# The order of the head work beside a hybrid encoder layer's dense matmuls, and where its short convolution is computed

## The chip, the cores and the metric

The kernel runs on one core of one Trainium2 chip. The metric is the device time of one launch in microseconds; below it, a profile of one execution tells where the time goes. TensorE (PE) does matmuls and transposes, VectorE (DVE) and GpSimd (POOL) elementwise work, ScalarE (ACT) activations and copies, and SyncE (SP) issues the transfers between the chip's memory and the core's. Each engine takes its own instructions in order and waits at one whose inputs are not there.

## The reference

One layer over a prompt of 2048 tokens and a sample group of 32 tokens with carried-in states; the model width is 1024, all values are float32.

```python
hn = rmsnorm(h, norm_mix)
qkv_pre, z, ba, u5, cc = split(hn @ w_in)
ya = gdn_mixer(...)        # delta rule: 4 heads x 128
yb = s5_mixer(...)         # diagonal state space, scan
yc = conformer_conv(...)   # gate, 31-tap causal conv, layernorm, silu
h = h + concat(ya, yb, yc) @ w_out
hf = rmsnorm(h, norm_ffn)
h = h + (silu(hf @ w1) * (hf @ w3)) @ w2
h = h + (p @ pe_w) * sigmoid(h @ pe_gate)
y = rmsnorm(h, norm_final)
```

`gdn_mixer` first passes q, k and v (1536 channels) through a causal convolution of width 4 and a silu, normalises q and k, and then runs a gated delta rule over chunks: within a chunk a triangular system is solved, from chunk to chunk a 128 x 128 state per head is carried. The kernel uses chunks (windows) of 128 tokens. All states are outputs too.

## The kernel before, in words

Tokens are taken in four blocks of 512; the last block also has the 32 sample tokens (544). All dense products are done as three passes of rounded parts: each operand is split into a high and a low part, and high x high, low x high and high x low are added up (`_dense`, line 122 of the profile: 24 matmuls of 512 columns for one 128-column tile of a weight with eight row tiles). `load_weight` loads a weight tile, ScalarE makes the high part (L94), GpSimd (for w3 VectorE) the low one (L98); the low parts are kept in device memory (L102), and later blocks load them (L93) instead of computing them.

**Phase A** (`PhaseA.block`, four blocks) computes the input projection, 22 weight tiles a block: first the two u5 tiles, then the conformer's gate and value (ccg, cca, two tiles each), twelve qkv tiles (`PhaseA.conv`), and four z tiles. The norm's factor comes late: its sums run beside the first tiles, and a broadcast of it over the partitions, `bc`, is made on TensorE after the first u5 tile (L134). Every result but u5's is multiplied by it when it leaves PSUM. `conv` writes a tile's product into `raw` (L615). For blocks 0 and 1 it then does the width-4 convolution at once (one ScalarE copy, L623, and three VectorE steps, L625) and the silu (L627, L628) and stores the result in `sild`; for blocks 2 and 3, which are in `G.raw`, it stores the raw rows.

**Phase F** (`PhaseF.block`, four blocks) does the output projection (8 tiles), the feed-forward part (22 hidden tiles of w1 and w3, L1194 to L1202; w2 in groups of four hidden tiles, L1216), the gated embedding (L1239 to L1241) and the final norm.

**The heads** are the work between the phases, one generator for each kind. `s5_init` prepares the constants of the state space. `gdn_of(b)` runs two delta-rule groups of two windows each for block b, and in block 3 a small third group for the sample. A group (`gdn_group`) loads its rows; for blocks in `G.raw` it does the convolution and silu itself (L887 to L892); then come the norms of q and k (L905), the products of keys (L933), the transposes of v (L957), a trip through device memory (`ud`, `cu`), 31 elimination steps of two small VectorE operations each (L980, L981), a trip back (`xd`, `X`), a VectorE transpose into `XT` (L990), two doublings on TensorE (L1011 q, L1024 z, L1042), and for each window the products with the state (L1054, L1067, L1074, L1081, L1082), and last the normalised output (L1107, L1108), stored to `mixT`. `conf_of(b)` is the conformer: 31 taps over two channel tiles, all on VectorE in one accumulator per tile (L822, L824), transposes (L835), layer norm, transposes back (L854). `s5_of(u)` does two blocks of the state space.

**What sets the order.** A generator yields between its parts. `dense` calls `step` with its columns, and each time STAGE columns of dense work have been issued, every chain in `G.chains` is advanced by one part; a `yield n` holds its chain for n parts. Chains share the right side of the memory: the pools of one kind reuse the space of another, so a kind starts when the one whose space it takes is finished. Phase A's block 0 is issued first; then a first chain is started: `s5_init`, `gdn_of(0)`, `conf_of(0)`. A second chain, `s5_of(0)`, starts before block 2. After phase A, `G.flush()` issues all that is left of the chains. In phase F one chain runs `conf_of(b)`, `s5_of` (at b = 2) and `gdn_of(b)` for b = 1, 2, 3, and before each F block a flush finishes what that block reads.

The program issued in this way is not yet the order on the engines. A planner with its own timing model orders each engine's instructions by priority and by when its model finds them ready: loads, evictions and splits go first ("first"), the dense matmuls and the heads share one lower priority ("later"), in which the place in the program counts.

```python
G.acc += cols
while G.acc >= STAGE:
    G.acc -= STAGE
    G.chains = [c for c in G.chains if advance(c)]
```

Of the kernel before, what the change touches and what calls it, by code (L numbers as in the profile page):

```python
# [8 lines left out]
F32 = mybir.dt.float32  # L9
F32R = mybir.dt.float32r  # L10
AF = mybir.ActivationFunctionType
# [5 lines left out]
P = 128  # L17
# [12 lines left out]
STAGE = 9216  # L30
# [541 lines left out]
class PhaseA:  # L572
# [60 lines left out]
    def block(self, b):  # L633
# [38 lines left out]

        for j in range(2):
# [3 lines left out]
            u = wp.tile([P, L5, n // L5], F32, tag="gacc", name="u5")  # L677
# [3 lines left out]
            if j == 0:  # L681

                with G.later():
                    bcast_cols(G, G.psN, "pn", rc, n, bc)
                    pb = G.psN.tile([P, 512], F32, tag="pn", name="ps_ba")
                    for w in range(4):
                        nc.tensor.transpose(pb[:, w * 16:(w + 1) * 16], fb[:, w * P:(w + 1) * P], G.ident[:16, :16])
                    if last:
                        nc.tensor.transpose(pb[:TS, 64:80], fb[:, BLK:n], G.ident[:16, :16])
                    pb3 = pb[:, :80].rearrange("p (w c) -> p w c", c=16)  # L690
                    ba = wp.tile([P, 4, 8], F32, tag="ba", name="ba")
                    bl = wp.tile([P, 5, 8], F32, tag="bl", name="bl")
                    nc.scalar.activation(bl[:, :4], pb3[:, :4, 8:], AF.Copy)
                    V.tensor_tensor(ba, pb3[:, :4, :8], bl[:, :4], op=ALU.add)
                    V.tensor_tensor(ba, ba, rc[:, :4, None].to_broadcast([P, 4, 8]), op=ALU.mult)
                    if last:
                        bad = wp.tile([TS, 1, 8], F32, tag="bad", name="bad", bufs=1)
                        nc.scalar.activation(bl[:TS, 4], pb3[:TS, 4, 8:], AF.Copy)
                        V.tensor_tensor(bad[:, 0], pb3[:TS, 4, :8], bl[:TS, 4], op=ALU.add)
                        V.tensor_scalar(bad, bad, rt, None, op0=ALU.mult)  # L700
                    gs = [gates(G, A, wp, G.psN, ba, b * 4, [P, 4, 8], "gp", G.tp_)]
                    if last:
                        gs.append(gates(G, A, wp, G.psN, bad, 0, [TS, 1, 8], "gd", G.td_))
                    for g in gs:
                        next(g)
# [96 lines left out]
def conformer_block(G, A, b, wp, pspool):  # L802
# [18 lines left out]
    for j in range(2):  # L821
        V.tensor_scalar(acc[:, j], xc[:, j, 0:W], cn_.w[:, j, 0:1], cn_.b[:, j:j + 1], op0=ALU.mult, op1=ALU.add)  # L822
        for t in range(1, TAPS):
            V.scalar_tensor_tensor(acc[:, j], xc[:, j, t:t + W], cn_.w[:, j, t:t + 1], acc[:, j], op0=ALU.mult, op1=ALU.add)  # L824
            if t % 6 == 0:
                yield 1
# [737 lines left out]
```

## Time and profile before

| what | us |
|---|---|
| median of three runs | 2949.75 (2946.05 to 2954.26) |
| the profiled execution | 2947.25 |
| its span, first to last instruction | 2945.4 |
| PE busy | 2769.4 |
| DVE busy | 1764.2 |
| ACT busy | 938.9 |
| POOL busy | 534.5 |
| mean granted TensorE clock | 0.969 |

The profile's times are microseconds from the first instruction; "mean" durations are nanoseconds. A row of a group reads: line, engine, operation, tile written <- tiles read, shape, xcount | busy, mean of one | idle time of the engine just before them and what ended it. A row of the timeline reads: start, duration, engine, line, operation, count, and in brackets how long the engine stood idle before it and for what. The table of busy times by stage gives the busy time of each engine in a stretch with the count of its instructions, then the granted clock and the share of the transfer engines. Matmuls overlap in the profile, so their mean duration is longer than the distance between two of them.

### The profile page before, as it was taken

The numbers are of one execution on the slowest core, as the hardware profiler recorded it, in microseconds if no ns is written. First come the engines' busy times: TensorE is split into PE (matmuls) and PEld (weight loads), VectorE is DVE, ScalarE is ACT, GpSimd is POOL, SyncE is SP. The second block draws the span as 40 slices with busy tenths as digits, with TensorE's granted clock in tenths as the row PEclk, the third lists the DMA queues.
The fourth block names the chain that finished last, engine by engine and source line by source line (L and its number), as shares of the span: only waits on it lengthen the run. The fifth ranks groups of instructions, "written<-read, shape, count | busy, mean of one in ns | idle before, by whom it ended". The sixth has DMA issues, their size and how long they took to land.

```text
span 2945.4 us, 40970 instructions
## 1 busy us (share of the span) xinstructions
PE 2769.4 (94%) x15300; PEld 2364.0 (80%) x15300; DVE 1764.2 (60%) x3933; ACT 938.9 (32%) x1409; POOL 534.5 (18%) x460
## 2 busy tenths in 40 slices
PE   7799999992999999799999999999999979999997
PEld 5678787992878878588788887778888869999997
DVE  8966737478675766966474664956374643333343
ACT  4243422221422222243332333342242423222232
POOL 5731213022332422441010010101010110000000
PEclk9899999995999999999999999999999979999998
DMA  6587767662654646487665565666555554555553
GB/s 221 168 291 263 237 213 222 196 197 80 228 173 167 205 157 212 136 282 212 205 199 177 191 193 175 233 203 181 177 187 176 186 192 155 179 175 172 172 183 106
DMA packets 278919, 565.32 MB, mean 192 GB/s; under 512 B 67344, under 2 KB 126880, under 8 KB 278576
## 3 DMA queue, kind: packets, MB, share of 16 engines
q1 hardware_dynamic: 278720, 562.70, 59.3%
q8 instruction: 121, 1.98, 0.3%
q14 instruction: 78, 0.64, 0.1%
HBM read 457.76 MB, written 104.25 MB: 191 GB/s over the span
## 4 chain that ended last, share of the span: by engine, by line
PE 69%; DVE 14%; DMA 8%; issue 5%; ACT 1%; SPq 1%; POOL 1%; DVEq 0%; ACTq 0%; POOLq 0%
PE ps_d L122 60%; DVE cacc L824 4%; DMA xk<-in_xT 1%; DVE cx L981 1%; DMA mixT<-zy 1%; DVE gacc L625 1%; PE ps_kk L933 1%; DVE ct L980 1%; PE ps_q L1011 1%; PE ps_z L1024 1%; DMA cu<-ud 1%; PE ps_o L1081 1%; PE ps_o L1082 1%; PE ps_vn L1067 1%; DVE hb L1216 1%
## 5 line engine op out<-in xcount | busy, mean ns | idle before, releaser
L94 ACT ACTIVATE wh_w<-wr_w 128x1024 fp32r<-128x1024 f32 (+1 forms) x272 | 281.2, 1034 | 766.2 <-PE ps_d L122 528.7
L122 PE MATMUL ps_d<-fah,wh_w 128*128 128x512 f32 (+1 forms) x1760 | 378.1, 354 | 6.7 <-DVE fa L1194 3.0
L122 PE MATMUL ps_d<-fal,wh_w 128*128 128x512 f32 (+1 forms) x1760 | 379.3, 354 | 0.0
L122 PE MATMUL ps_d<-fah,wl_w 128*128 128x512 f32 (+1 forms) x1760 | 377.8, 353 | 0.0
L122 PEld LDWEIGHTS ps_d<-fah,wh_w 128*128 128x128 f32 x1760 | 291.2, 189 | 51.9 <-DVE fa L1194 3.4
L122 PEld LDWEIGHTS ps_d<-fal,wh_w 128*128 128x128 f32 x1760 | 291.9, 189 | 43.7 <-issue 0.5
L122 PEld LDWEIGHTS ps_d<-fah,wl_w 128*128 128x128 f32 x1760 | 291.4, 189 | 42.7
L1216 DVE TENSOR_TENSOR hb<-hb,ps_d 128x512 f32<-128x512 f32 (+1 forms) x240 | 139.7, 584 | 170.9 <-PE ps_d L122 170.3
L122 PE MATMUL ps_d<-acth,wh_w 128*128 128x512 f32 (+1 forms) x880 | 209.6, 355 | 17.8 <-DVE hb L1216 13.7
L122 PE MATMUL ps_d<-acth,wl_w 128*128 128x512 f32 (+1 forms) x880 | 209.7, 354 | 0.0
L122 PE MATMUL ps_d<-actl,wh_w 128*128 128x512 f32 (+1 forms) x880 | 207.5, 353 | 0.0
L824 DVE SCALAR_TENSOR_TENSOR cacc<-xc,cc_w,cacc 128x512 f32<-128x512 f32 (+1 forms) x240 | 194.4, 858 | 0.0
L122 PEld LDWEIGHTS ps_d<-acth,wh_w 128*128 128x128 f32 x880 | 147.7, 189 | 46.0 <-DVE hb L1216 12.9
L122 PEld LDWEIGHTS ps_d<-acth,wl_w 128*128 128x128 f32 x880 | 149.1, 189 | 22.4
L122 PEld LDWEIGHTS ps_d<-actl,wh_w 128*128 128x128 f32 x880 | 149.1, 188 | 22.3
L98 POOL TENSOR_TENSOR wl_w<-wr_w,wh_w 128x1024 fp32r<-128x1024 f32 (+1 forms) x46 | 111.3, 2421 | 269.4 <-ACT wh_w L94 238.5
L1194 DVE TENSOR_TENSOR fa<-ps_d,bc 128x512 f32<-128x512 f32 (+1 forms) x110 | 64.7, 589 | 131.6 <-PE ps_d L122 123.2
L1199 DVE SCALAR_TENSOR_TENSOR fth<-ps_d,bc 128x512 f32<-128x512 f32 (+1 forms) x110 | 64.7, 589 | 129.8 <-PE ps_d L122 129.3
L122 PE MATMUL ps_d<-hh,wh_qkv 128*128 128x512 f32 (+1 forms) x480 | 109.1, 368 | 13.8 <-DVE raw L615 13.7
L1197 DVE SCALAR_TENSOR_TENSOR fa<-fth,fa 128x512 f32<-128x512 f32 (+1 forms) x110 | 74.0, 674 | 58.7 <-ACT fth L1196 58.6
L122 PE MATMUL ps_d<-hh,wl_qkv 128*128 128x512 f32 (+1 forms) x480 | 105.5, 361 | 2.6 <-POOL wl_qkv L98 2.1
L1201 ACT ACTIVATE acth<-fa 128x512 fp32r<-128x512 f32 (+1 forms) x110 | 60.3, 548 | 143.0 <-DVE fa L1200 142.8
(479 smaller groups left out, 4785.2 us busy)
## 6 DMA issues: line engine op xcount, KB each, us to landing
wr_w<-in_w SPq DMA_DIRECT2D x256, 512.0 KB, 4.2
wl_w<-lo_w SPq DMA_DIRECT2D x192, 512.0 KB, 4.0
lo_w<-wl_w SPq DMA_DIRECT2D x64, 512.0 KB, 2.9
wr_qkv<-in_w_in SPq DMA_DIRECT2D x48, 512.0 KB, 4.9
wl_qkv<-lo_qkv SPq DMA_DIRECT2D x36, 512.0 KB, 4.7
wr_out<-in_w_out SPq DMA_DIRECT2D x32, 512.0 KB, 4.5
wr_gate<-in_pe_gate SPq DMA_DIRECT2D x32, 512.0 KB, 4.7
wl_out<-lo_out SPq DMA_DIRECT2D x24, 512.0 KB, 4.6
```

Of the source, the lines that this page charges most:

```text
L94: nc.scalar.activation(wh, wr, AF.Copy)
L98: e.tensor_tensor(wl, wr, wh.bitcast(F32), op=ALU.subtract)
L122: nc.tensor.matmul(ps[:, :cn], a[:, i, :], x(k)[:, c0:c0 + cn], start=start and p_ == 0 and i == 0, stop=stop and p_ == 2 and i == K - 1)
L625: V.scalar_tensor_tensor(acc, raw[:, t:t + W], cw[:, m, t:t + 1], acc, op0=ALU.mult, op1=ALU.add)
L824: V.scalar_tensor_tensor(acc[:, j], xc[:, j, t:t + W], cn_.w[:, j, t:t + 1], acc[:, j], op0=ALU.mult, op1=ALU.add)
L933: nc.tensor.matmul(kk4[:, h - h0], kq[:, 2 * h, cw], kq[:, 2 * h:2 * h + 2, cw], start=True, stop=True)
L980: V.tensor_tensor(t, cx[:, 0:nq, j:j + 1].to_broadcast(sh), cu[:, j:j + 1, j + 1:].to_broadcast(sh), op=ALU.mult)
L1194: V.tensor_tensor(a, p1[:, :cn], bc[:, cs], op=ALU.mult)
L1197: V.scalar_tensor_tensor(a, th, 1.0, a, op0=ALU.add, op1=ALU.mult)
L1199: V.scalar_tensor_tensor(th, p3[:, :cn], 0.5, bc[:, cs], op0=ALU.mult, op1=ALU.mult)
L1201: nc.scalar.activation(fa[:, cs], a, AF.Copy)
L1216: V.tensor_tensor(hb[m][:, c0:c0 + cn], hb[m][:, c0:c0 + cn], p_[:, :cn], op=ALU.add)
```

## The change

Six edits:

1. STAGE becomes a table: 6144 columns in phase A and in F blocks 1 to 3, 8192 in F block 0 (it was 9216 everywhere), so a part follows more closely on the last.
2. The conformer yields after every fourth tap instead of every sixth: 18 parts instead of 14.
3. In the first chain `conf_of(0)` comes before `gdn_of(0)`.
4. `G.raw` holds all four blocks: in phase A, blocks 0 and 1 store raw rows as well, and their delta-rule groups do the convolution and silu. Such a group has 40 parts instead of 32.
5. In phase A both u5 tiles are issued before the broadcast of the norm's factor and the gate work; their two `raw` buffers are held until it is there.
6. The last block's gates move with it; nothing else of them changes.

```diff
-STAGE = 9216
+STAGE = {"A": 6144, 0: 8192}
...
+        urs = []
         for j in range(2):
             w = load_weight(G, A.w_in[16 + j], KD, "u5", j)
...
-            if j == 0:
-                with G.later():
-                    bcast_cols(G, G.psN, "pn", rc, n, bc)
...
+            urs.append(ur)
+        with G.later():
+            bcast_cols(G, G.psN, "pn", rc, n, bc)
...
+        for j, ur in enumerate(urs):
+            u = wp.tile([P, L5, n // L5], F32, tag="gacc", name="u5")
             V.tensor_tensor(u, ur.rearrange("p (c s) -> p s c", s=L5), bc.rearrange("p (c s) -> p s c", s=L5), op=ALU.mult)
...
-            if t % 6 == 0:
+            if t % 4 == 0:
                 yield 1
...
-        while G.acc >= STAGE:
-            G.acc -= STAGE
+        while G.acc >= G.stage:
+            G.acc -= G.stage
...
+    G.stage = STAGE["A"]
...
-    G.raw = set(range(2, NB))
+    G.raw = set(range(NB))
...
+                yield from conf_of(0)
                 yield from gdn_of(0)
-                yield from conf_of(0)
...
     for b in range(NB):
         G.flush(lambda: ready[0] >= b)
+        G.stage = STAGE.get(b, STAGE["A"])
         pf.block(b)
```

More of the change, by code (lines that the diff above doesn't have):

```diff
@@ L676, in block @@
             ur = wp.tile([P, n], F32, tag="raw", name="u5r")
-            u = wp.tile([P, L5, n // L5], F32, tag="gacc", name="u5")
             for c0, cn in chunks_of(n):
@@ L680, in block @@
                 nc.scalar.activation(ur[:, c0:c0 + cn], p_[:, :cn], AF.Copy)
-            if j == 0:
-                with G.later():
-                    bcast_cols(G, G.psN, "pn", rc, n, bc)
[L685 to L705, printed above, removed]
@@ new lines, in block @@
+            urs.append(ur)
+        with G.later():
+            bcast_cols(G, G.psN, "pn", rc, n, bc)
+            pb = G.psN.tile([P, 512], F32, tag="pn", name="ps_ba")
+            for w in range(4):
+                nc.tensor.transpose(pb[:, w * 16:(w + 1) * 16], fb[:, w * P:(w + 1) * P], G.ident[:16, :16])
+            if last:
+                nc.tensor.transpose(pb[:TS, 64:80], fb[:, BLK:n], G.ident[:16, :16])
+            pb3 = pb[:, :80].rearrange("p (w c) -> p w c", c=16)
+            ba = wp.tile([P, 4, 8], F32, tag="ba", name="ba")
+            bl = wp.tile([P, 5, 8], F32, tag="bl", name="bl")
+            nc.scalar.activation(bl[:, :4], pb3[:, :4, 8:], AF.Copy)
+            V.tensor_tensor(ba, pb3[:, :4, :8], bl[:, :4], op=ALU.add)
+            V.tensor_tensor(ba, ba, rc[:, :4, None].to_broadcast([P, 4, 8]), op=ALU.mult)
+            if last:
+                bad = wp.tile([TS, 1, 8], F32, tag="bad", name="bad", bufs=1)
+                nc.scalar.activation(bl[:TS, 4], pb3[:TS, 4, 8:], AF.Copy)
+                V.tensor_tensor(bad[:, 0], pb3[:TS, 4, :8], bl[:TS, 4], op=ALU.add)
+                V.tensor_scalar(bad, bad, rt, None, op0=ALU.mult)
+            gs = [gates(G, A, wp, G.psN, ba, b * 4, [P, 4, 8], "gp", G.tp_)]
+            if last:
+                gs.append(gates(G, A, wp, G.psN, bad, 0, [TS, 1, 8], "gd", G.td_))
+            for g in gs:
+                next(g)
```

## The prediction

> **What bounds the kernel now.** First the page: busy shares, and the row of PE in 40 slices of 73.6 us. Then the busy times by stage, which I cut where the profile shows the stages change.
>
> ```profile
> PE 2769.4 (94%) x15300; PEld 2364.0 (80%) x15300; DVE 1764.2 (60%) x3933; ACT 938.9 (32%) x1409; POOL 534.5 (18%) x460
> PE   7799999992999999799999999999999979999997
> ```
>
> ```profile
> core 0: us, PE busy (x) PEld busy (x) DVE busy (x) ACT busy (x) POOL busy (x), PEclk, DMA share, GB/s
> 0.00:185.00 185.00, 151.11 (x624) 116.27 (x625) 166.45 (x397) 66.09 (x98) 107.10 (x109) 0.93 0.65 218
> 185.00:675.00 490.00, 475.31 (x2844) 407.67 (x2842) 307.78 (x822) 158.78 (x252) 99.95 (x153) 0.99 0.72 223
> 675.00:735.00 60.00, 9.71 (x33) 5.06 (x34) 47.58 (x88) 7.91 (x15) 9.44 (x11) 0.52 0.17 58
> 735.00:1285.00 550.00, 528.74 (x2473) 430.24 (x2473) 380.91 (x621) 168.86 (x241) 187.45 (x89) 0.98 0.55 185
> 1285.00:1836.00 551.00, 545.42 (x2695) 449.59 (x2693) 314.19 (x760) 190.32 (x278) 60.47 (x46) 1.00 0.65 202
> 1836.00:2372.00 536.00, 527.39 (x2522) 431.80 (x2522) 340.63 (x813) 187.79 (x287) 46.48 (x36) 0.99 0.61 194
> 2372.00:2406.00 34.00, 13.57 (x57) 8.45 (x55) 13.61 (x28) 4.52 (x7) 6.60 (x5) 0.58 0.41 140
> 2406.00:2945.00 539.00, 518.19 (x4062) 514.88 (x4062) 193.09 (x410) 154.64 (x235) 17.05 (x12) 0.97 0.51 168
> ```
>
> The stages: phase A block 0 (to 185), A blocks 1 to 3 (to 675), a hole, phase F blocks 0 to 2, a second hole, F block 3. TensorE fills 97 to 99% of the four long stages in the middle and stands mostly idle in three places: block 0 (34 us of 185), the hole of 60 us, the hole of 34 us. Only there is time to be had without taking work from TensorE, and the change takes none. The timeline of TensorE and its waits say what the holes are:
>
> ```profile
> 713.89 1.35 PE L835 MATMUL ps_ct<-ident,cacc 128*128 128x128 f32 x4 [38.97 <-DVE cacc L824]
> 734.76 7.42 PE L122 MATMUL ps_d<-fah,wh_out 128*128 128x512 f32 x22
> ...
> 2399.59 0.63 PE L1107 MATMUL ps_ot<-ident,o 32*128 32x32 f32 x4 [10.10 <-DVE o L1099]
> 2405.95 6.16 PE L122 MATMUL ps_d<-fah,wh_out 128*128 128x272 f32 x22 [5.73 <-ACT fah L1132]
> ```
>
> The first hole is the conformer of block 0: nothing dense is left, and its convolution runs on VectorE alone. The second is the sample's delta-rule group, last of the heads for F block 3. Block 0 waits for VectorE:
>
> ```profile
> PE ps_d L122 <- DVE raw L615: 14.3, 4, 6.1
> ```
>
> ```profile
> 33.69 0.63 PE L122 MATMUL ps_d<-hh,wh_cca 128*128 128x512 f32 x2
> 39.39 1.05 PE L134 MATMUL ps_bc<-ident,rso 128*128 128x128 f32 x4 [5.07 <-issue]
> ...
> 112.36 3.75 PE L122 MATMUL ps_d<-hh,wh_qkv 128*128 128x512 f32 x8 [6.06 <-DVE raw L615]
> ```
>
> **The part arithmetic.** A chain advances one part (one yield; yield 2 is two) per STAGE columns of dense work. A block of phase A has 22 tiles x 24 matmuls x 512 = 270,336 columns, the last 287,232; a block of F 1,032,192. Counting yields: s5_init 15, the conformer 14, a two-window delta-rule group 32, or 40 where it does its own convolution, the sample's group 28, an S5 unit 46, the last 48. Before: the first chain needs 15+64+14 = 93 parts, and blocks 1 to 3 (827,904 columns) give 89.8 of 9216: the conformer, last, falls into the flush. In F, 78+142+122 = 342 parts meet 3 x 112 = 336: the second hole. After: 15+18+80 = 113 parts against 134.8 of 6144; in F 98+146+126 = 370 against 126+168+168 = 462, and each block's own target is met (98 of 126; 244 of 294). S5 unit 0 has 46 of 90.7. So both flushes should find nothing to do, with 21 parts to spare in A. The price of a part on TensorE is dense time:
>
> ```profile
> 1524.17 1.02 PE L933 MATMUL ps_kk<-kq 128*128 128x256 f32 x4
> ...
> 1559.29 2.00 PE L122 MATMUL ps_d<-fah,wl_w 128*128 128x512 f32 x8
> 1561.13 2.00 PE L122 MATMUL ps_d<-fal,wh_w 128*128 128x512 f32 x8
> ...
> 1573.57 1.89 PE L1011 MATMUL ps_q<-XT,U 128*128 128x64 f32 x16
> ```
>
> ```profile
> 1570.56 1.25 DVE L990 STREAM_TRANSPOSE XT<-X 128x1024 f32<-128x1024 f32 x1 [5.04 <-DMA X<-xd]
> ```
>
> Eight matmuls are 1.84 us apart, 0.23 each: a part is 18 x 0.23 = 4.14 us now, 12 x 0.23 = 2.76 after, 16 x 0.23 = 3.68 in F block 0.
>
> **Terms**, against the profiled execution's 2947.25 us (span 2945.4 plus 1.85; the median of the runs, 2949.75, is 2.5 above it).
>
> ```profile
> L625 DVE SCALAR_TENSOR_TENSOR gacc<-raw,cw,gacc 128x512 f32<-128x512 f32 x36 | 37.2, 1035 | 1.4 <-ACT gacc L623 1.1
> L628 DVE SCALAR_TENSOR_TENSOR gacc<-gth,gacc 128x512 f32<-128x512 f32 x12 | 13.2, 1096 | 1.6 <-ACT gth L627 1.5
> ```
>
> ```profile
> L824 DVE SCALAR_TENSOR_TENSOR cacc<-xc,cc_w,cacc 128x512 f32<-128x512 f32 x120 | 87.9, 786 | 0.0
> L625 DVE SCALAR_TENSOR_TENSOR gacc<-raw,cw,gacc 128x512 f32<-128x512 f32 x36 | 27.7, 768 | 7.8 <-ACT gacc L623 7.2
> L628 DVE SCALAR_TENSOR_TENSOR gacc<-gth,gacc 128x512 f32<-128x512 f32 x12 | 9.4, 781 | 3.9 <-ACT gth L627 3.9
> ```
>
> 1. *Block 0 loses its convolution* (first two rows, up to 185 us): 37.2 + 13.2 = 50.4 us of the 166 us of VectorE. The four waits for raw (14.3) go, and the slow matmuls behind them: after the one of 6.06 us, eight took 3.75 us instead of 2.00 (the row at 112 us and, below, the one at 1559), so some 7 for four. VectorE's lag costs more than its marked waits: of the stage's 34 idle us only 5 are the broadcast's, which stay, since the norm's chain sets them. Late next is GpSimd with 107 us of work. I take 27: 14 and 7, and 6 of the other 15 idle us; 35 if nearly all of them go, 10 if GpSimd's weights are late instead. The raw rows go out by the same 12 stores, sooner than now; behind them on the DMA queue stand the weights of later tiles, so that can only help. -27 (-10 to -35).
>
> 2. *The first hole.* 60 us, less the conformer's own matmuls (9.7 at half clock, some 6 at full) that now run among dense ones, and less a start of F block 0 of 6: the F2 row below has 3.57 of wait and 18 matmuls in 7.40 instead of 4.1. -48 (-40 to -54).
>
> ```profile
> 1835.67 7.40 PE L122 MATMUL ps_d<-fah,wh_out 128*128 128x512 f32 x18 [3.57 <-ACT fah L1132]
> ```
>
> 3. *What A blocks 1 to 3 take up.* The conformer of block 0 goes ahead of the group: one load, two stores, its GpSimd normalisation and 60 taps x 0.786 = 47 us into block 1, which loses 27.7 + 9.4 = 37 us. The group gains:
>
> ```profile
> L889 DVE SCALAR_TENSOR_TENSOR kq<-rawX,cw,kq 128x256 f32<-128x256 f32 x48 | 21.1, 478 | 2.1 <-ACT kq L887 2.1
> L892 DVE SCALAR_TENSOR_TENSOR kq<-cth,kq 128x1024 f32<-128x1024 f32 x8 | 9.7, 1218 | 0.6 <-ACT cth L891 0.5
> ```
>
> Two groups x (36 x 0.478 + 3 x 1.218) = 41.7 us a block, 24 copies and 6 tanh on ScalarE, three loads for two. VectorE then has 308 - 37 + 42 + 48 = 361 us in some 490 (48: what it did in the hole). The clear of X on GpSimd waits for the convolution, and the copies of the tails and the norms' roots queue behind it, as the next raw tile does behind those; GpSimd is busy 100 of 490 us here and makes no weights, and a tile's 24 x 0.23 = 5.5 us hide it; without that cover it is a few us a group. The u5 edit issues the broadcast one tile later: nothing, or the few us of PE's waits at it. 0 (-10 to +15).
>
> 4. *F block 0 takes block 1's convolution.* VectorE is slower here, and by the end of the stage full:
>
> ```profile
> L824 DVE SCALAR_TENSOR_TENSOR cacc<-xc,cc_w,cacc 128x512 f32<-128x512 f32 x60 | 60.8, 1054 | 0.0
> ```
>
> ```profile
> 1200.00:1225.00 25.00, 17.09 (x63) 12.03 (x61) 25.00 (x26) 8.42 (x12) 14.83 (x8) 0.93 0.45 156
> ```
>
> At 1054/786 the 41.7 us become 56: 381 + 56 = 437 of 550. GpSimd computes the low halves of the weights here, 187 us; the clear of X stands before some of them. Where VectorE is full TensorE loses 8 us in 25; some 30 us of the 56 falling in such places would cost 10. +10 (0 to +46). The Trainium skill's GPSIMD Engine Reference (Key points) says GpSimd contends with VectorE instructions that have two SBUF inputs, which speaks against moving this work here and not into A; the two tap rows agree. By that rule alone, with all 56 us beyond cover, the total would be 46 higher.
>
> 5. *The second hole*: 34 us, less 8 of matmuls that stay and 3 of start. -23 (-18 to -28).
>
> 6. *Closer parts.* From the last kk row to q are 12 parts, 49 us; XT is written 1.8 us before q. The chain between (scratch out and in, 62 small VectorE operations, out and in again) needs 46.6 us whatever the parts are, and 12 parts will be 33 us, or 44 in F block 0. If q stayed at its place, TensorE, which takes instructions in order, would wait 13.5 us, with all dense work behind it. But the planner places an instruction when its own model has it ready. The broadcast (39.39 us, above) comes ahead of the ccg and cca tiles in the program, and was put behind the first of them and two matmuls of the second. So what is left is the model's error. VectorE shows it, with 8 large groups:
>
> ```profile
> DVE XT L990 <- DMA X<-xd: 29.9, 8, 6.3
> DVE ct L980 <- DMA cu<-ud: 27.9, 8, 6.2
> ```
>
> 3.7 and 3.5 us a group, 7.2 together; TensorE itself lags the plan, so I take 2 us for each of 8 groups: +16 (0 to +58, all of it at each). The Trainium skill's TensorE: Matmul & The Clock Gate (What's actually happening) halves the clock after an idle window of about 3.4 us; the first matmuls after both holes agree. By it, waits beyond 3.4 us would add up to 1.7 us each, 14 in all.
>
> Sum: -27 - 48 + 0 + 10 - 23 + 16 = -72: 2875 for the profile, **2878** for the median.
>
> **Rivals.** *(a) The parts outrun the delta rule: slower.* The planner leaves q about where the program has it. Then 13.5 us x 6 groups (two in A, four in F) + 2.4 x 2 = 86, and the some 11 other handovers of a group, each 1.38 us shorter, half of that: 11 x 6 x 0.69 = 45. Terms 1 to 5 are -88; with +131: 2949.75 + 43 = 2993. It decides from 88/8 = 11 us of TensorE waits a group. For it: the slack of 1.8 us, and that engines keep their order. Against: the broadcast row. Chance 0.10. *(b) The first chain is not done at the end of A.* The delta rule is last there now; its two groups have chains of 46.6 us that closer parts don't shorten. The spare 21 parts are 60 us of dense work; twice 13.5 fits in. If 25 us stick out: 2903. Chance 0.07. *(c) VectorE becomes the bound in F block 0*: 46 more, 2924; chance 0.13. The stage table speaks for it (381 us already, slow taps), its mean share against it. *The forecast*: 0.70.
>
> **Range.** The holes are nearly certain gains (-58 to -82 together), the unknown ones are terms 1, 4 and 6. Low: term 1 and 6 at their good ends, -8 and -16, and some of 3: 2835. High: (b), (c) and a third of term 6's bad end: 2935; outside stays (a) and a little more. A measurement can tell about 0.3%, 9 us. Faster by more: nearly all of the forecast, (b), (c): 0.84; within: the worst of (c) and mild (a), 0.06; slower: 0.10.
>
> **What would show it.** Right: no TensorE wait of over 8 us around 640 to 670 us and none before F block 3; the first F matmul at about 660 instead of 735; the waits for raw in block 0 gone, block 0 ending near 158; the last group's matmuls in the first half of F block 2. Term 4: taps and L889 above 0.6 us in F block 0. Term 6: TensorE waits on XT, Q, X, vn of 1 to 4 us. Wrong: TensorE waits on the group's tiles summing to over 60 us, or a hole left at the end of A, or VectorE at over 95% through F block 0.

## The result and the profile after

| what | before | after |
|---|---|---|
| median of the runs, us | 2947.90 (4 runs, 2943.06 to 2954.26) | 2924.94 (4 runs, 2923.33 to 2926.11) |
| ratio, 95% interval | | 0.992 (0.990 to 0.9941) |
| profiled execution, us | 2947.25 | 2926.03 |
| its span, us | 2945.4 | 2924.2 |

The change makes the kernel 0.8% faster: 23 us by the medians, 21 by the profiled executions. That lies within the range, but it is less than a third of the 72 us forecast. Block 0 went as foreseen. Of the two holes the first got shorter and the second stayed, and a third one opened.

The page of the changed kernel, busy shares and the row of PE in 40 slices (73.1 us each):

```profile
PE 2763.8 (95%) x15300; PEld 2362.9 (81%) x15300; DVE 1768.2 (60%) x3993; ACT 940.2 (32%) x1421; POOL 534.7 (18%) x460
PE   7899999996999999899999996999999979999997
```

The dip of slice 10 is 6 where it was 2, the one of slice 33 is still a 7, and slice 25 has become a 6. Busy times by stage, cut at the new dips (same columns as before):

```profile
core 0: us, PE busy (x) PEld busy (x) DVE busy (x) ACT busy (x) POOL busy (x), PEclk, DMA share, GB/s
0.00:163.00 163.00, 136.56 (x556) 105.99 (x557) 138.04 (x351) 48.92 (x69) 93.00 (x109) 0.95 0.70 235
...
664.00:700.00 36.00, 14.23 (x104) 12.58 (x103) 16.71 (x44) 8.86 (x15) 7.17 (x7) 0.77 0.31 101
...
1806.00:1823.00 17.00, 4.56 (x14) 3.68 (x15) 4.18 (x6) 1.90 (x3) 1.28 (x1) 0.50 0.55 171
...
2372.00:2386.00 14.00, 1.46 (x7) 1.27 (x8) 6.43 (x13) 1.31 (x2) 3.00 (x4) 0.50 0.66 227
```

TensorE's waits, and its timeline at the three dips:

```profile
PE ps_d L122 <- ACT fah L1134: 32.0, 6, 13.0
PE ps_ot L1109 <- DVE o L1101: 25.3, 4, 10.1
PE ps_d L122 <- DVE xc L723: 12.5, 2, 6.8
...
PE ps_d L122 <- DVE raw L615: 6.6, 1, 6.6
```

```profile
684.50 1.97 PE L1109 MATMUL ps_ot<-ident,o 128*128 128x128 f32 x8 [6.29 <-DVE o L1101]
699.45 7.28 PE L122 MATMUL ps_d<-fah,wh_out 128*128 128x512 f32 x21 [12.98 <-ACT fah L1134]
...
1806.40 1.97 PE L1109 MATMUL ps_ot<-ident,o 128*128 128x128 f32 x8 [8.64 <-DVE o L1101]
1820.41 3.81 PE L122 MATMUL ps_d<-fah,wh_out 128*128 128x512 f32 x9 [12.04 <-ACT fah L1134]
...
2378.70 0.63 PE L1109 MATMUL ps_ot<-ident,o 32*128 32x32 f32 x4 [10.10 <-DVE o L1101]
2385.18 1.83 PE L122 MATMUL ps_d<-fah,wh_out 128*128 128x272 f32 x6 [5.84 <-ACT fah L1134]
```

All three have one shape: the last transpose of a delta-rule group (`ps_ot`) waits for its normalised `o`, then the output projection of the next F block waits for its input (`fah`), which this transpose completes. The first hole is no longer the conformer (39 us of wait for `cacc` before) but the delta rule of block 0, which is last now. The one before F block 2 is new (3.57 us of wait for fah before). The one before F block 3 is unchanged.

To compare kernels I cut each at two marks: the first matmul of the norm's sums of F block 0 (`ps_ss`, L151) and that of F block 3. What lies behind the second took 478.9 us before and 478.7 after.

| kernel | to F block 0's norm | from there to F block 3's | span |
|---|---|---|---|
| before | 790.0 | 1676.5 | 2945.4 |
| changed | 756.4 | 1689.1 | 2924.2 |

So phase A with the start of F gained 33.6 us, and F blocks 0 to 2 lost 12.6.

### The profile page after: what moved, and what is told of

Read it like the earlier page. It is cut to its first block, busy times and chain, and to the rows that moved or that the text cites. A ratio compares the mean times of both kernels' runs of the same rounds, so it can differ in the third digit from the quotient of the medians.

```text
span 2924.2 us, 41013 instructions
## 1 busy us (share of the span) xinstructions
PE 2763.8 (95%) x15300; PEld 2362.9 (81%) x15300; DVE 1768.2 (60%) x3993; ACT 940.2 (32%) x1421; POOL 534.7 (18%) x460
## 4 chain that ended last, share of the span: by engine, by line
PE 71%; DVE 9%; DMA 4%; issue 1%; ACT 1%; SPq 1%; POOL 0%; DVEq 0%; ACTq 0%; POOLq 0%
PE ps_d L122 63%; DVE cacc L826 2%; DVE kq L891 1%; PE ps_kk L935 1%; PE ps_q L1013 1%; PE ps_z L1026 1%; DVE hb L1253 1%; DVE vf L891 1%; DMA hb<-mixT 1%; PE ps_vn L1069 1%; PE ps_s L1076 0%; DMA rawAQ<-sild 0%; PE ps_o L1084 0%; PE ps_o L1083 0%; DVE ct L982 0%
## 5 line engine op out<-in xcount | busy, mean ns | idle before, releaser
L1204 DVE TENSOR_TENSOR actl<-fa,acth 128x512 fp32r<-128x512 f32 (+1 forms) x110 | 84.1, 765 | 49.0 <-ACT acth L1203 48.7
L94 ACT ACTIVATE wh_qkv<-wr_qkv 128x1024 fp32r<-128x1024 f32 x48 | 50.8, 1058 | 187.6 <-PE ps_d L122 154.1
```

The source lines that it names most:

```text
L94: nc.scalar.activation(wh, wr, AF.Copy)
L1204: V.tensor_tensor(fb[:, cs], a, fa[:, cs].bitcast(F32), op=ALU.subtract)
```

## Experiments

**Theory C (the chain).** The heads from one F block to the next are one serial chain: conformer, S5 unit, two delta-rule groups. STAGE is only the least distance of its parts; its pace is set by how one step waits for the last. The chain is about as long as the dense work beside it, and what makes it longer is paid where a block must wait for it. **Rival S** is the prediction's: STAGE sets the pace. **Rival V**: VectorE's load in F block 0 is what the moved convolution costs. What speaks for C in the trace of the changed kernel is the distance of a group's products in F block 1, where STAGE is 6144 columns, 12 matmuls:

```profile
1586.40 1.14 PE L1026 MATMUL ps_z<-X,Q 64*64 64x64 f32 x16
1587.47 0.96 PE L122 MATMUL ps_d<-fah,wl_w 128*128 128x512 f32 x3
1588.27 2.00 PE L122 MATMUL ps_d<-fal,wh_w 128*128 128x512 f32 x8
1590.11 2.00 PE L122 MATMUL ps_d<-fah,wh_w 128*128 128x512 f32 x8
1591.94 1.05 PE L1056 MATMUL ps_ks<-S,kq 128*128 128x128 f32 x8
1592.84 0.60 PE L1063 MATMUL ps_kt<-ident,kq 128*128 128x128 f32 x4
1593.19 2.10 PE L122 MATMUL ps_d<-fah,wl_w 128*128 128x512 f32 x8
1595.13 2.00 PE L122 MATMUL ps_d<-fal,wh_w 128*128 128x512 f32 x8
1596.97 2.00 PE L122 MATMUL ps_d<-fah,wh_w 128*128 128x512 f32 x8
1598.81 1.05 PE L1069 MATMUL ps_vn<-rk,X 128*128 128x128 f32 x8
```

Between z and ks lie 3 + 8 + 8 = 19 dense matmuls, between ks and vn 24. TensorE waits at none of these steps: they stand that far apart in its order of instructions.

### e1: STAGE alone

```diff
-STAGE = 9216
+STAGE = 6144
```

> The kernel before with only its STAGE changed, 6144 columns everywhere. Theory C (the heads of F blocks 0 to 2 are one serial chain with a pace of its own, 18 to 24 dense matmuls between one product of a delta-rule group and the next, which STAGE does not set): in phase A the chain has slack, so the conformer of block 0 comes before the end of A and the first hole of 60 us shrinks to about 10; in F the groups keep their length (about 160 us from the key products to the last transpose) and the hole before F block 3 stays at 30 us or more. Total about 2903, and block 0 as before. Rival S (STAGE sets the pace of the parts, as the prediction had it): the groups in F are a third shorter and the second hole goes as well; total about 2880.

Measured 2896.31 (2894.09 to 2902.49; ratio 0.9828, 0.9805 to 0.9851): 50 us gained, more than twice what the whole change gains. To F block 0's norm 743.6, then 1670.1. On its timeline F's second output matmul stands at 675 behind a wait of 2.88 us, and the hole before F block 3 is there as before:

```profile
674.71 5.05 PE L122 MATMUL ps_d<-fah,wh_out 128*128 128x512 f32 x14 [2.88 <-DVE zz L741]
...
2347.01 0.63 PE L1107 MATMUL ps_ot<-ident,o 32*128 32x32 f32 x4 [10.10 <-DVE o L1099]
2353.44 6.51 PE L122 MATMUL ps_d<-fah,wh_out 128*128 128x272 f32 x22 [5.80 <-ACT fah L1132]
```

C is right on both holes. The first hole of the kernel before was not one conformer's alone: the 124 taps of blocks 0 and 1 share VectorE there, from 604.6 to 714.5 us. In e1 those of block 0 have it to themselves and run from 581.3 to 628.1. The rest of the change takes back more than half of this edit's gain.

### e2: the changed kernel without edit 4

```diff
-    G.raw = set(range(NB))
+    G.raw = set([2, 3])
```

> The changed kernel with its edit 4 undone: the short convolution and silu of blocks 0 and 1 are done in phase A again. Theory C: block 0 takes back its 20 us and A stays as it is else, but the chain in F is some 17 us shorter, so the hole before F block 2 (about 20 us of waits) closes; the one before F block 3 stays. Net between -10 and +10 of the changed kernel, about 2920. Rival S and my prediction (the convolution is nearly free in F, 10 us): 27 lost, 10 won, about 2942. Rival V (VectorE bounds F block 0): F block 0 itself, first matmul to final norm, gets shorter by 20 us or more, which shows at its own end and not before block 2.

Measured 2918.78 (2912.4 to 2921.52; ratio 0.9894, 0.9867 to 0.992): 6 below the changed kernel, with intervals that overlap. The sums of A block 1's norm start at 203.2 instead of 177.5, F block 0's at 766.6 instead of 756.4, and F blocks 0 to 2 take 1674.5 instead of 1689.1. So edit 4 wins 25.7 in block 0, loses 25.7 - 10.2 = 15.5 in the rest of A and 14.5 in F: nothing is left. F block 2 starts without a wait:

```profile
1814.40 4.10 PE L122 MATMUL ps_d<-fah,wh_out 128*128 128x512 f32 x14
```

F block 0 itself, from its first output matmul to its final norm, takes 562.7 us here and 559.7 in the changed kernel, with 388.5 and 408.7 us of VectorE: the price of the convolution isn't paid there, and V is refuted by this pair. (From output norm to final norm it is 506.7 and 502.7, but part of the moved work lies ahead of that mark.)

One more difference shows here. From A block 1's norm to F block 0's e1 takes 543.3 us and e2 563.4, though both compute the convolution of blocks 0 and 1 in phase A. These 20 us go with edits 2, 3 and 5 and the first steps of F block 0 at 8192 columns; no run here takes them apart.

### e3: closer parts in F

```diff
-STAGE = {"A": 6144, 0: 8192}
+STAGE = {"A": 6144, 0: 3072, 1: 3072, 2: 3072, 3: 3072}
```

> The changed kernel with STAGE 3072 in all F blocks (8192 and 6144 there) and the same phase A. Theory C: groups of the same length, 150 to 165 us; the chain gains only where it waited for its next part between groups in F block 0; the hole before F block 3 stays (TensorE waits for o of 8 us or more there). Total 2900 to 2920. Rival S: parts half as far apart, both holes of F gone, 2885 or less, or TensorE waits for the group's tiles that sum to over 60 us if they outrun the chain.

Measured 2916.40 (2913.75 to 2919.03; ratio 0.9893, 0.9871 to 0.9915). The hole before F block 3 stays:

```profile
2373.19 1.80 PE L122 MATMUL ps_d<-fah,wh_out 128*128 128x272 f32 x6 [13.43 <-ACT fah L1134]
```

The first group of F block 1, from its first norm product to its last transpose. The rows are those of one line of one kernel each, with the start of the first and the last instruction; before (9216 columns):

```profile
L905 PE MATMUL ps_nrm<-ones,qsq x16: 164/250/250, 1501.9 to 1503.4; 128*128 128x1 f32 x16
...
L1107 PE MATMUL ps_ot<-ident,o x8: 270/272/273, 1661.7 to 1662.5; 128*128 128x128 f32 x8
```

the changed kernel (6144):

```profile
L907 PE MATMUL ps_nrm<-ones,qsq x16: 167/250/250, 1489.0 to 1490.6; 128*128 128x1 f32 x16
...
L1109 PE MATMUL ps_ot<-ident,o x8: 272/272/273, 1649.3 to 1650.1; 128*128 128x128 f32 x8
```

and e3 (3072):

```profile
L907 PE MATMUL ps_nrm<-ones,qsq x16: 166/250/250, 1449.2 to 1450.8; 128*128 128x1 f32 x16
...
L1109 PE MATMUL ps_ot<-ident,o x8: 270/272/273, 1605.8 to 1606.6; 128*128 128x128 f32 x8
```

159.8, 160.3 and 156.6 us. There are 30 parts between these marks; at 4.14, 2.76 and 1.38 us each they would be 124, 83 and 41. For this group rival S is out.

At the start of F block 0 it is not. There the parts of the conformer come first, then the convolution and the first key products (`ps_kk`) of a group. These products in F block 0, in the changed kernel (8192 columns there) and in e3 (3072):

```profile
L935 PE MATMUL ps_kk<-kq x16: 378/379/379, 767.6 to 832.1; 128*128 128x256 f32 x16
```

```profile
L935 PE MATMUL ps_kk<-kq x16: 377/379/462, 746.3 to 767.7; 128*128 128x256 f32 x16
```

F's first output matmul stands at 699.45 and at 696.50, so the last of them comes 133 us behind it in the changed kernel and 71 in e3, with the same parts. And the hole before F block 2 is gone in e3: from F block 1's final norm to F block 2's output norm it takes 46.3 us, 85.9 in the changed kernel, 53.7 before. So the distance alone can close that hole. Little of it stays in the total, because head work that ran there now runs beside dense work: F block 0's norm comes 9.8 us later, and from F block 0's final norm to F block 1's output norm it takes 17.7 us more.

### e4: four PSUM buffers of one kind

The heads have two kinds of PSUM buffers (TensorE writes its products to these), "pc" for the conformer and the state space and "pm" for the delta rule, two of each (the expectation below names the kinds less exactly). Here they share four; the layout of the rest stays.

```diff
-    G.psM = E("psm", 2, space=PSUM)
+    G.psM = E("psm", 4, space=PSUM)
...
-        p_ = pspool.tile([P, 512], F32, tag="pc", name="ps_ct")
+        p_ = pspool.tile([P, 512], F32, tag="pm", name="ps_ct")
```

(and the same for `ps_cf`, `ps_cfd` and the state space's `ps_pt`, `ps_kg`, `ps_v`, `ps_y`, `ps_glu`)

> The changed kernel with one kind of four PSUM buffers for all heads instead of two kinds of two (the conformer's and the others'). STAGE and all the work are the same. Theory C with its pace set by the two buffers that all products of a group share: the handovers of a group come closer, a group from key products to last transpose 20 us or more shorter, both holes in F close, total about 2885; the hole at the end of A stays. If the pace is set by the engines' own latencies instead: groups as long as before, total 2917 to 2933.

Measured 2882.56 (2879.47 to 2888.06; ratio 0.978, 0.9757 to 0.9803), 42 below the changed kernel. The same group of F block 1:

```profile
L907 PE MATMUL ps_nrm<-ones,qsq x16: 168/250/250, 1486.4 to 1488.0; 128*128 128x1 f32 x16
...
L1109 PE MATMUL ps_ot<-ident,o x8: 272/272/273, 1624.9 to 1625.7; 128*128 128x128 f32 x8
```

138.5 us: 21.8 less with the parts where they were. Both holes of F are gone; before F block 3 the output projection runs without a wait:

```profile
2348.36 1.14 PE L122 MATMUL ps_d<-fah,wh_out 128*128 128x272 f32 x7
```

To F block 0's norm 760.0, then 1648.3. The buffers are thus a part of the pace, 22 of 160 us; ks, vn and s still stand some 20 dense matmuls apart. That the planner's spacing of dependent steps makes the rest is likely and not shown. The Trainium skill's Perfetto Trace Analysis (Matmul Optimizations) asks to make use of all eight PSUM banks. All eight were given out here before too (three for the dense products, one for the norms, two and two for the heads), but two of them to a kind that the delta rule doesn't use; sharing those is worth the 42 us above in the changed kernel, which agrees with the rule, and nothing in the total of e9 below.

### e5 to e8: one edit undone, or one alone

e5, edit 3 undone:

```diff
-                yield from conf_of(0)
                 yield from gdn_of(0)
+                yield from conf_of(0)
```

> The changed kernel with its edit 3 undone: the delta rule of block 0 comes before its conformer again. Theory C (one serial chain of heads, paid for where a block of F must wait for it): the order inside the first chain doesn't change the length of the chain, only what is last at the end of A; the hole there is some 20 us either way (the conformer then starts about 55 us of dense work before the end, and takes 60 taps of 0.79 us and its tail), and F blocks 0 to 2 wait as in the changed kernel. 2915 to 2935. Rival O (the order closes the first hole, the prediction's term 2): the hole returns to 40 us or more; 2945 or more.

Measured 2931.49 (2926.96 to 2933.69; ratio 0.9953, 0.9936 to 0.997), 6.5 above the changed kernel, with intervals that overlap a little. The hole at the end of A is the conformer's again, but a short one: 11.61 us of wait for `cacc`, where it was 39.0 before. F block 0's norm starts 5.2 us later than in the changed kernel (761.6), F block 1's 4.8 later (1309.2): the rest of F is the same. C holds; the rival that the order closes the hole does not.

e6, the kernel before with edit 5 alone (the lines on `urs` in the diff of the change):

> The kernel before with edit 5 alone: both u5 tiles ahead of the broadcast of the norm's factor. If the new wait of 6.8 us for the gate's input in block 0 of the changed kernel comes from this edit, it shows here and the total rises by 3 to 7 us; if it comes from the lighter VectorE of block 0 (TensorE gets to the gate sooner), it does not show, and the total stays within 4 us of the kernel before.

Measured 2944.48 (2939.57 to 2947.53; ratio 0.9996, 0.9985 to 1.0008): nothing. The wait for `xc` is 1.48 us here:

```profile
54.71 2.13 PE L122 MATMUL ps_d<-hh,wh_cca 128*128 128x512 f32 x8 [1.48 <-DVE xc L723]
```

So the 6.8 us in the changed kernel don't come from this edit alone; e7, with edit 4 alone, waits 3.15 us, the kernel before 2.22. In all four the matmul behind the wait starts between 54 and 56 us, so block 0 isn't longer by it. What makes the wait longer is not shown.

e7, the kernel before with edit 4 alone:

```diff
-    G.raw = set(range(2, NB))
+    G.raw = set(range(NB))
```

> The kernel before with edit 4 alone: all blocks store raw rows. Theory C: block 0 gains its 20 us, but the groups of blocks 0 and 1 get 8 parts more at 9216 columns, so part of the delta rule of block 0 falls behind the end of A with the conformer (hole 60 to 90 us), and the chain in F is 17 us or more longer, so a new hole opens before F block 2. Net 2945 to 2975, no gain or a loss. Rival (the prediction's own terms for this edit, -27 and +10): about 2930.

Measured 2970.89 (2968.83 to 2971.64; ratio 1.0084, 1.0065 to 1.0103): 0.8% slower. A block 1's norm starts at 179.4 (197.7 before), F block 0's at 810.0 (790.0): the first hole has taken the gain and 20 us more.

```profile
725.82 1.35 PE L835 MATMUL ps_ct<-ident,cacc 128*128 128x128 f32 x4 [51.41 <-DVE cacc L824]
```

e8, edit 1 undone:

```diff
-STAGE = {"A": 6144, 0: 8192}
+STAGE = {"A": 9216}
```

> The changed kernel with edit 1 undone: STAGE 9216 everywhere. Theory C: the first chain now has 113 parts for some 90 stages, so the second delta-rule group of block 0 runs after the end of A with nothing dense beside it: a hole of 100 us or more; in F the groups keep their length, only conf(1), conf(2) and the S5 unit are later, so the hole before F block 2 grows by 15 to 45 us; total 2990 to 3030. If STAGE matters little in A as well, the total stays within 20 us of the changed kernel.

Measured 2975.58 (2972.4 to 2977.92; ratio 1.0099, 1.0075 to 1.0122): slower than before, by less than C said. To F block 0's norm 792.3, then 1703.8. The first group of block 0 takes 183.3 us here (384.6 to 567.9) and 172.3 in the changed kernel (348.2 to 520.5): a part a third shorter makes a group 6% shorter. F's first output matmul stands at 737.05, 38 us later than in the changed kernel, behind the same two waits and one of 26 us for `XT` ahead of them. The later half of block 0's second group falls behind the last dense matmul of phase A here, and that shows what a group's steps take by themselves:

```profile
688.40 3.65 PE L1013 MATMUL ps_q<-XT,U 128*128 128x64 f32 x16 [26.42 <-DVE XT L992]
...
722.10 1.97 PE L1109 MATMUL ps_ot<-ident,o 128*128 128x128 f32 x8 [6.69 <-DVE o L1101]
```

From the first q to the last transposes it is 33.7 us, with no dense matmul between. The first group of F block 1 in the changed kernel takes 86.3 us for the same steps (from the row below to 1649.3), with some 300 dense matmuls between; at 0.23 us each these are 69.

```profile
1562.97 1.89 PE L1013 MATMUL ps_q<-XT,U 128*128 128x64 f32 x16
```

So more than half of that stretch is the dense work put between the steps, and not the time that the steps need.

### e9: the buffers at 9216 columns

The edit of e4 on the kernel before.

> The kernel before (STAGE 9216) with one kind of four PSUM buffers for all heads. Theory C, as it now stands (a handover takes the larger of two distances: the next part, STAGE columns later, and the next free PSUM buffer; at 9216 columns, 18 matmuls, both are alike): the buffers alone bring little, both holes of before stay (60 and 34 us), total 2935 to 2950. If the buffers alone set the pace: the hole before F block 3 goes, total 2920 or less.

Measured 2955.58 (2945.52 to 2958.87; ratio 1.0029, 1.0017 to 1.0042): no gain, even 0.3% slower; TensorE still waits 39.0 us for the conformer. To F block 0's norm 793.2, then 1682.7. But C was wrong on the hole before F block 3: it is gone, as the rival had it, and the output projection there hardly waits:

```profile
2410.40 1.83 PE L122 MATMUL ps_d<-fah,wh_out 128*128 128x272 f32 x6 [0.52 <-ACT fah L1132]
```

The first group of F block 2 takes 141.5 us, 160.3 before, and from F block 2's final norm to F block 3's output norm it takes 71.0 us, 86.4 before. From F block 0's norm to F block 1's, though, it takes 22.0 us more than before (579.4 against 557.4), and no run shows why. The groups of F block 1 are not shorter (160.4 and 149.3 us, 159.9 and 138.9 before). So at this distance the buffers close one hole and gain nothing in total; in e4 and e14, with closer parts, they gain.

### e10: a shorter chain ahead of F block 2

The changed kernel leaves out 60 of the 62 taps of block 2's conformer here.

```diff
         for t in range(1, TAPS):
-            V.scalar_tensor_tensor(acc[:, j], xc[:, j, t:t + W], ...)
+            if b != 2:
+                V.scalar_tensor_tensor(acc[:, j], xc[:, j, t:t + W], ...)
```

> The changed kernel with 60 of the 62 convolution taps of the conformer of block 2 left out (its output for that block is not the layer's); the parts stay where they are. Theory C: the chain is some 60 us shorter ahead of the delta rule of block 2, so the hole before F block 2 closes and TensorE's waits for o and fah at about 1806 to 1820 us go; the hole before F block 3 lies behind another conformer and stays. Total 2895 to 2915. If the hole before F block 2 comes from the PSUM buffers alone or from VectorE's load, it stays and the total is within 8 us of the changed kernel.

Measured 2892.69 (2886.22 to 2894.97; ratio 0.9816, 0.98 to 0.9833), 32 below the changed kernel, a little more than expected. F block 2 starts without a wait, F block 3 waits as ever:

```profile
1797.07 1.77 PE L122 MATMUL ps_d<-fah,wh_out 128*128 128x512 f32 x7
...
2353.48 5.87 PE L122 MATMUL ps_d<-fah,wh_out 128*128 128x272 f32 x22 [13.45 <-ACT fah L1135]
```

This is plain evidence for the chain: 60 VectorE steps less in F block 0, TensorE's own work unchanged, and what goes is the hole at the end of the block after (85.9 us from final norm to output norm, now 46.3). The edit also lightens VectorE: F block 0 itself, output norm to final norm, is 10 us shorter (492.6 against 502.7), so a part of the 32 us may be VectorE's and not the chain's.

### e11 to e13: all holes at once, three misses

e11 is the changed kernel with e4's buffers and e5's order and these two lines:

```diff
-STAGE = {"A": 6144, 0: 8192}
+STAGE = {"A": 3072}
...
-    G.raw = set(range(NB))
+    G.raw = set([0, 2, 3])
```

e12 is the kernel before with e4's buffers and STAGE = 3072; e13 is e11 with 4608 for 3072.

> The changed kernel with the delta rule of block 0 ahead of its conformer again, the convolution of block 1 back in phase A (raw rows for blocks 0, 2 and 3), STAGE 3072 everywhere and the four PSUM buffers. Theory C: block 0 keeps its 20 us, the first hole shrinks to about 10, neither F block 2 nor F block 3 waits for the heads; from the kernel before -20 -45 -25 and a few us back in A: about 2860 (2850 to 2875). Rival (closer parts make TensorE wait for the group's tiles): waits for q, z, vn, s, o that sum to over 40 us, total 2880 or more.

> The kernel before with two edits only: STAGE 3072 and the four PSUM buffers. Theory C: block 0 as before, the first hole about 10, no hole in F: 2945 -45 -25 = 2875 (2865 to 2890), more than three times the gain of the whole change. If the gain of the four buffers in the changed kernel hung on its other edits: 2895 or more.

> As e11 (delta rule first, raw rows of blocks 0, 2 and 3, four PSUM buffers), but STAGE 4608 for 3072 everywhere. In e11 the S5 unit of blocks 0 and 1 was last at the end of A (15.4 us of wait for gq, at about 680 to 695). Theory C with that correction (at 3072 columns two chains crowd VectorE, and the S5 unit, second in each stage, falls behind): at 4608 the S5 unit, the delta rule and the conformer are all done before A ends, no wait for gq, the first output norm of F at about 730 (781 in e11, 756 in the changed kernel), no hole in F: total 2850 to 2870. If the hole of e11 comes from A having too much head work for its dense work in any order, the first hole stays at 30 us or more and the total at 2885 or above.

| kernel | median, us | ratio | to F block 0's norm | from there to F block 3's |
|---|---|---|---|---|
| e11 | 2920.88 (2917.71 to 2926.43) | 0.9919 (0.9904 to 0.9934) | 780.9 | 1665.7 |
| e12 | 2934.13 (2933.95 to 2937.09) | 0.996 (0.9945 to 0.9976) | 795.3 | 1662.0 |
| e13 | 2889.43 (2888.18 to 2894.71) | 0.9824 (0.9811 to 0.9838) | 761.4 | 1646.6 |

All three came out above their ranges, by 46, 44 and 19 us. F has no hole before blocks 2 and 3 in any, as was said. The misses lie mostly at the end of A. In e11 and e12 the S5 unit, which runs beside the first chain, is last; the row is e11's:

```profile
695.62 5.52 PE L556 MATMUL ps_glu<-gq,glu 128*128 128x512 f32 x8 [15.36 <-DVE gq L546]
```

In e13 it is done in time, as expected, but the conformers of blocks 0 and 1 then meet there (120 taps from 578.6 to 693.5 us), and TensorE waits for them:

```profile
685.66 0.69 PE L856 MATMUL ps_cf<-ident,ctk 128*128 128x128 f32 x2 [12.51 <-POOL ctk L853]
```

Which head is last at the end of A changes from kernel to kernel; that one is late does not.

### e14 to e16: which edits to keep

e14 is the kernel before with e1's and e4's edits. e15 is e4 with these lines:

```diff
-STAGE = {"A": 6144, 0: 8192}
+STAGE = {"A": 6144}
...
-    G.raw = set(range(NB))
+    G.raw = set([0, 2, 3])
```

e16 is the changed kernel with e4's buffers, e5's order and e2's `G.raw = set([2, 3])`: beside e14 it has 8192 columns in F block 0, and edits 2 and 5.

> The kernel before with STAGE 6144 and the four PSUM buffers, and nothing else. Theory C: the first hole as in e1 (some 10 us), and the hole before F block 3 that e1 kept (24 us above its cover) gone: 2896 - 23 = about 2873 (2865 to 2882). If the four buffers pay only against the longer chain of the changed kernel: 2890 or more.

> e4 (the changed kernel with four PSUM buffers) with the convolution of block 1 back in phase A, and STAGE 6144 in F block 0 as well. Theory C: in e4 F block 0 to 2 don't wait for the chain any more, so a chain shorter by that convolution gains nothing beside a few us: 2874 to 2888. Rival V (the convolution costs F block 0 by VectorE's load): F block 0, from its output norm to its final norm, is 15 us or more shorter than in e4 (505) and the total is below 2870.

> e14 (delta rule first, convolutions of blocks 0 and 1 in A, 6144 columns, four PSUM buffers) with edits 1, 2 and 5 of the change as they are, so above all with 8192 columns in F block 0 where e14 has 6144. In e14 F block 0 took 526 us from output norm to final norm, in e4 with 8192 columns 505. If the head work packed into F block 0 costs it that (rival V in another form: VectorE, with slow taps there, holds up the evictions), F block 0 is back at about 505 and the total at 2860 to 2870; if not, the total stays within 6 us of e14.

| kernel | median, us | ratio | to F block 0's norm | from there to F block 3's |
|---|---|---|---|---|
| e14 | 2878.76 (2877.97 to 2883.29) | 0.9783 (0.977 to 0.9797) | 734.0 | 1664.5 |
| e15 | 2891.53 (2889.86 to 2893.87) | 0.9824 (0.9811 to 0.9837) | 758.2 | 1654.5 |
| e16 | 2869.13 (2868.01 to 2872.64) | 0.9743 (0.9728 to 0.9758) | 741.4 | 1646.3 |

e14 came out as said (2873): the buffers need nothing of the change but its STAGE. e16 gains 10 us more and is the fastest of all kernels tried, 76 us below the one before; F block 0 takes 508.5 us in it, 526.1 in e14. So 8192 columns there are probably worth having; e16 has edits 2 and 5 as well, and no run takes the three apart. The cause that e16's expectation gave, VectorE, isn't shown: of the 17 us longer stage of e14, TensorE is busy for 11 (500.35 against 488.92, with 59 matmuls more), which is work done earlier, not waiting. e15 came out some 4 above its range: F block 0 takes 516.9 us with less convolution in it and 504.6 in e4 with more. That is the opposite of what V says, but e15 also has e14's 6144 columns there, and the 10 us between e14 and e16 cover its 9 against e4; the clean pair against V is e2 and the changed kernel.

### e17 and e18: two more misses

e17 puts the conformer of block 1 behind that of block 0, in its buffers; e18 is e17 with `G.raw = set([0, 2, 3])`.

```diff
-                yield from conf_of(0)
+                with R("cc_0") as wp:
+                    yield from conf(0, wp)
+                    yield from conf(1, wp)
...
-            yield from conf_of(b)
+            if b > 1:
+                yield from conf_of(b)
```

> e16, with the conformer of block 1 in the same buffers as that of block 0, so that its convolution can't begin before the first has ended. In the kernel before, the two share VectorE at the end of A (120 taps from 605 to 714 us), which makes the first one last twice as long. Theory: the first output norm of F comes some 5 to 10 us earlier than in e16, total 5 to 10 lower. Rival: the end of A is already covered, no difference (within 5 us).

> e17 with the raw rows of block 0 kept (edit 4 for block 0 alone): block 0 gains 20 to 25 us, and the delta rule of block 0 does its own convolution in blocks 1 to 3. If the first chain has slack there, the total falls by 20 below e17. Theory C, by e13 (block 0 ends 25 us earlier than in e14, the first output norm of F is 27 us later): what block 0 gains is handed back at the end of A, because the chain that starts earlier is longer by the same; total within 10 us of e17.

Measured 2907.45 (2901.78 to 2912.2; ratio 0.9865, 0.9845 to 0.9885) and 2942.22 (2934.81 to 2947.31; ratio 0.9994, 0.9982 to 1.0005): 38 and 73 above e16. In e17 the transposes of block 0's conformer come 19 us earlier (613.7 instead of 632.6), as meant. But block 1's is now issued by the flush ahead of F's first tile, and TensorE, in order, waits for it and then for fah:

```profile
682.28 2.12 PE L837 MATMUL ps_ct<-ident,cacc 128*128 128x128 f32 x8 [6.60 <-DVE cacc L826]
...
703.31 7.29 PE L122 MATMUL ps_d<-fah,wh_out 128*128 128x512 f32 x22 [10.98 <-ACT fah L1134]
```

So e17 swapped one cost for another, and its total says nothing on the sharing of VectorE. e18 against e17 is a clean pair for block 0's raw rows: A block 1's norm 25.7 us sooner (177.4 against 203.1), F block 0's 35.2 later (805.5 against 770.3), with both conformers late:

```profile
693.33 0.69 PE L856 MATMUL ps_cf<-ident,ctk 128*128 128x128 f32 x2 [18.97 <-POOL ctk L853]
...
717.95 1.94 PE L837 MATMUL ps_ct<-ident,cacc 128*128 128x128 f32 x8 [20.02 <-DVE cacc L826]
```

"Within 10 us" was wrong; the 25.7 us that block 0 gains are handed back more than twice over (60.9 us), where the end of A has no slack.

## Why the prediction was right in sign and wrong in size

**The step that failed** is the part arithmetic: "A chain advances one part per STAGE columns", and from it "both flushes should find nothing to do, with 21 parts to spare in A". STAGE says only when a part is issued at the earliest. In the first group of F block 1, 30 parts took 160, 160 and 157 us at 9216, 6144 and 3072 columns. The comparison was at hand in the trace of before: those 30 parts at 4.14 us are 124 us, and the group there took 159.8. The prediction itself noted that the planner places a step when its model has it ready, used that for term 6 and didn't carry it to terms 2 and 5. Where the distance does set the pace, at the start of F block 0, the arithmetic compared totals of parts and didn't ask when, after the block's first matmul, a given part is issued.

- Term 1, block 0 (-27): measured -20.2 (A block 1's norm 197.7 to 177.5), -25.7 by e2. Right, within its bounds. Of the waits for raw one of 6.6 us is left; the one for `xc`, 2.2 us before, is 6.8 now.
- Term 2, the first hole (-48): failed, in the way of rival (b), which was given 0.07. From A block 3's norm to F block 0's the time fell from 279.6 to 259.7, 20 us. Rival (b) had 25 us sticking out; the last transpose is at 684.5 and F's first matmul at 699.5, 35 behind the last dense one at about 664. That A had enough room was right: e1 shows -46 to the mark of F block 0 with the same STAGE there. The change fills the room: e2 measures 15.5 us for the convolution in A (e7 and e18 more), and e2 against e1 another 20 us for edits 2, 3 and 5 together (and F block 0's 8192 columns). The prediction's reading that block 0's conformer makes the first hole also missed that block 1's shares VectorE with it (`x120` in its own row).
- Term 3 (0): A blocks 1 to 3 gave back 6.5 us (block 1's to block 3's norm 312.7 to 319.2). Within its bounds.
- Term 4, F block 0 takes block 1's convolution (+10): the VectorE work was sized well (54.0 us for the rows of L891 and L894, 56 foreseen), but it costs the stage nothing: from F's first output matmul to F block 0's final norm it takes 560.7 us before and 559.7 after. VectorE, rival (c), was not the price. The price is the length of the chain, 14.5 us by e2, paid before F block 2.
- Term 5, the second hole (-23): failed, 0. The waits of 10.10 and 5.73 us are still there, 10.10 and 5.84. e1 and e3 show that STAGE alone, at these values, doesn't close it, e4 and e9 that shorter groups do.
- Term 6, closer parts (+16): no wait for a tile of a group beyond the `o` ones exceeds 5.3 us, and from F block 0's norm to F block 1's final one it is 15.9 us faster (1052.9 to 1037.0). Rival (a) did not show: there the parts don't drive the chain, so they can't outrun it.
- Missing in the list: the hole before F block 2. F block 1's final norm is 49.5 us earlier than before, F block 2's output norm 17.3: 32 us go in between. F starts 35 us sooner (699.45 against 734.76), but the last key products of the first group in F block 0 end where they did, at 832.1 us (832.5 before): 33 parts lead up to them instead of 21, by 4 parts of edit 2 and 8 of edit 4, and at 3.68 and 4.14 us a part that is 121 us instead of 87. The last transposes of F block 1's groups then come only 11 us sooner than before. Without the 8 parts (e2) or with closer ones (e3) the hole is gone. The prediction counted whether there were parts enough and never how long the chain takes from block to block.

The sum as measured: -20.2 + 6.5 - 19.9 = -33.6 up to F block 0's norm, +12.6 to F block 3's, -0.2 behind: -21.2. That this lies in the range is luck in part, for the ends of the range don't follow from what the prediction names for them: 2878 - 8 - 16, with term 3's 10, is 2844 and not 2835, and (b), (c) and a third of the 42 us left in term 6 make 2878 + 25 + 46 + 14 = 2963 and not 2935. The two holes, called nearly certain for 58 us or more, gave 20. One reading of the stages is a little off too: from 735 to 1285 us TensorE is busy for 96% (528.74 of 550), not 97.

The Trainium skill's TensorE: Matmul & The Clock Gate (What's actually happening), cited in the prediction for its halved clock after an idle window, again fits the trace: the clock granted in the two later holes is 0.50, and after 12.04 us of idling nine matmuls take 3.81 us where eight back to back take 2.00. Each hole costs a little more than its waits.

What stays open: why the steps of a group are put as far apart as they are (e8 shows only that from q on they need 34 of 86 us), which of edits 2, 3 and 5 costs the 20 us in A, and why F block 0 is longer at 6144 columns than TensorE's busy time explains.

## What to carry to other kernels

An interval at which steps are issued bounds a chain from one side only, and whether it binds can differ from stage to stage: take the duration of a whole chain from the trace, divide by its parts, and if that is more than the interval, look for what else the steps wait for (here the few PSUM buffers that all share) before counting on a shorter interval. Work moved off a full stage into a serial chain costs nothing only while the chain has slack at every point where someone waits for its end; here 25 us won in block 0 were paid back in full. Try the edits of a bundle singly: a shorter STAGE alone gave twice what the bundle gave (e1), and with a change of buffers that was not among the six edits nearly three times (e14).
